# A gate folded into the last quarter of the output weights, and the last block stored in three pieces

## The chip, the cores and the metric
The kernel runs on one core of one Trainium2 chip. A core has TensorE (PE: matmuls, and the loads of their stationary operands, PEld), VectorE (DVE), ScalarE (ACT), GpSimd (POOL) and SyncE (SP); each runs its own instructions in order and they wait for one another by semaphores. SP, ACT and POOL also issue DMAs, which sixteen DMA engines carry out. The metric is the device time of one execution in microseconds (us). The kernel before took 1354.91 us, the median of three runs (1353.6 to 1355.62).

## The reference, cut to what matters
The program is a two-layer hybrid network over 256 latent tokens and 256 context tokens of width 1024: layer 0 mixes tokens with an mLSTM, layer 1 with latent attention, and each is followed by a gated feed-forward part with a short convolution. What the change touches is the very end, the feed-forward part of layer 1 for the latent tokens:

```python
def _conv_ffn(h, w_in, conv_w, conv_b, w_out):
    gate, up = jnp.split(h @ w_in, 2, axis=-1)
    return (jax.nn.silu(_dwconv(gate, conv_w, conv_b)) * up) @ w_out
...
        f = _conv_ffn(_modulate(x, ml[3], ml[4]), ffn_w_in[i], ffn_conv_w[i], ffn_conv_b[i], ffn_w_out[i])
        x = _layer_norm(ALPHA * x + ml[5] * f, ln_g[i, 1], ln_b[i, 1])
```

`ml[5]` is a row of 1024 numbers, one for each output column, that comes from the condition `c`. It multiplies the columns of `f`, and `f` is a product with `w_out`; so multiplying the columns of `w_out` by it beforehand gives the same. The layer norm then takes mean and variance over the 1024 columns of each token and applies `ln_g` and `ln_b`.

## The kernel before, in words
All values are 32-bit. A matmul operand is held as the sum of a rounded high part and the rest, its low part, and a product is made of three matmuls (`mm3`, lines 417 to 422): high by high, high by low, low by high. Weights arrive as tiles of 128x1024, called raw (512 KB). `Stream` brings them in the order of a fixed list: `_load` (line 291) issues the load on SP into a ring of buffers, nine of them in the last part; `_split` (line 317) lets ScalarE round the raw tile to the high part (line 339), and `low` (line 359) lets VectorE subtract that from the raw tile (line 361), after which the raw buffer is free for the next load. Ordinary weights take one of three buffers of the tag `w`, so that the split of one waits until TensorE is done with the weight three before. Those marked wide take two buffers of another tag (`wu` in the profile) and are split ahead. `use` (line 368) hands a weight out and splits up to `AHEAD` = 8 further ones.

The layers' instructions are written down in program order, and a scheduler then orders those of each engine by priority (program order) and by when it reckons them ready. DMAs are subject to it too. Instructions marked `pin` keep their order.

In the feed-forward part of layer 1, `ffn_in` (line 1533) goes over 22 pairs of weights `fin1`. For each, TensorE makes a product, ScalarE and VectorE fetch it from the accumulators, apply the convolution and the activation, and split the result into `act`. Then `outmm` (line 1468) multiplies the 22 activations by the 22 weights `fout1`, one of 128x1024 for each. The 256 tokens are two blocks (t = 0 and 1) of 128. Block 0 has two accumulators of 512 columns, block 1 has three, of 512, 256 and 256 (`acc4(True)`, line 1491). The first 16 weights are each used for both blocks. The last six (`TAIL`, line 64) are kept, and used for one accumulator after another, so that these are finished one by one: block 0 first, columns 768 to 1023 of block 1 last. Of the 22, the first 12 are ordinary and the last ten wide (`WIDE`, line 65).

`ln_rows` (line 1179) follows: for each chunk, it multiplies the accumulator by the gate (line 1189), adds `ALPHA` times the residual (line 1190) and takes the statistics (line 1192). When the chunks of a block are in, it combines the statistics (line 1194), takes the root on ScalarE (line 1196) and the reciprocal, and a small product `nm` (line 1199). In this last call (`fin` given) the second pass subtracts the mean and multiplies by `ln_g` (line 1207), multiplies by the reciprocal root and adds `ln_b` (line 1209), in halves of 512 columns, and stores each half (line 1214): the first from SP, the second from ScalarE. The first half of block 0 goes another way, over ScalarE and POOL (lines 1211 to 1213).

The rows of gates are in memory as `gd[l, c]`, written by VectorE and SP (lines 539 to 543). `bcast` (line 1171) loads one from POOL's queue into all 128 partitions. `mask` (line 472) is a tile of 128x256 that only the mLSTM of layer 0 reads.

Of the kernel before, what the change touches and what calls it, by code (L numbers as in the profile page):

```python
# [11 lines left out]
ALU = mybir.AluOpType  # L12
# [11 lines left out]
ALPHA = float((2 * DEPTH) ** 0.25)  # L24
# [7 lines left out]
CW = 1024  # L32
# [34 lines left out]
MWIDE = (3, 4, 5, 6)  # L67

YTAIL = 3


def _stat(w, m, kt0, nkt):
# [10 lines left out]
def _plan():  # L83
    ids, order = {}, []

    def add(key, cols, wide=False):
        if key not in ids:
            ids[key] = (len(ids), cols)
        order.append((key, wide))
# [28 lines left out]
    for n in ("y21", "y22", "yt4"):  # L118
        for j in range(6):
            if (n, j) == ("yt4", 6 - YTAIL):  # L120
                for c, m in enumerate((3, 3, 2)):
                    add(("dkv", 0, c), m * 320)
            add((n, 0, j), cols[j], n == "yt4" and j >= 6 - YTAIL)
    for c in range(2):
# [129 lines left out]
class Stream:  # L254
# [62 lines left out]
    def _split(self):  # L317
        k, j = self.k, self.ns
        key, wide = self.order[j]
        cols = self.ids[key][1]  # L320
        while self.nl <= j:
            self._load()
        self.nsum = max(self.nsum, j)
        while self.nsum < min(j + SUMS, self.n):
            while self.nl <= self.nsum:
                self._load()
            self._sum(self.nsum)
            self.nsum += 1
        raw = self.raw[j]
        if wide:  # L330
            h, l = self.unit(), None
            if self.later is None:
                l = self.unit()
        else:
            w = k.pool.tile([128, 2, CW], F32R, tag="w", name="w", bufs=NB)
            h, l = w[:, 0], w[:, 1]
            self.live.append(j)
        src = raw[:, :cols]
        k.behind(k.nc.scalar.copy(h[:, :cols], src), self.behind)  # L339
        if key[0] in ("vt2", "yt2"):  # L340
            k.nc.scalar.dma_start(k.t2d[key[0][0], key[1], key[2]][:, :cols], src)
        self.hl[j] = [h, l]
        self.ns += 1
        if l is None:
            self.later.append((j, src, self.hl[j]))
        elif key[0] == "dkv" and key[2]:
            self.kept_low.append((j, src, h, l))
        else:
            self.low(j, src, h, l)
        while self._room():  # L350
            self._load()
# [39 lines left out]
class K:  # L391
# [787 lines left out]
    def ln_rows(self, pss, xres, gate, fin=None):  # L1179

        nc = self.nc
        self.zs = zs = []
        for t in range(2):
            z = self.uf("z")
            st = self.tiny(6 * len(pss[t]), "st").rearrange("p (a b) -> p a b", b=6)
            for i, (ps, c) in enumerate(pss[t]):
                h = c.start // 512
                hc = slice(c.start - h * 512, c.stop - h * 512)
                nc.vector.tensor_tensor(z[:, c], ps, gate[h][:, hc], op=ALU.mult)
                nc.vector.scalar_tensor_tensor(z[:, c], xres[t][h][:, hc], ALPHA, z[:, c],  # L1190
                                               op0=ALU.mult, op1=ALU.add)
                nc.vector.bn_stats(st[:, i], z[:, c])
            mv = self.tiny(2, "mv")
            nc.vector.bn_aggr(mv, st)
            rs = self.tiny(1, "rs")
            nc.scalar.activation(rs, mv[:, 1:2], AF.Sqrt, bias=self.keps, scale=1.0)
            nc.vector.reciprocal(rs, rs)
            nm = self.tiny(1, "nm")
            nc.vector.scalar_tensor_tensor(nm, mv[:, 0:1], -1.0, rs, op0=ALU.mult, op1=ALU.mult)
            fine = len(pss[1]) > 2  # L1200
            if fin is not None:
                g, b, out = fin
                for c0, c1 in ((0, 512), (512, 1024)):
                    c, h = slice(c0, c1), c0 // 512
                    hc = slice(c0 - h * 512, c1 - h * 512)
                    if t or c0 == 512:
                        nc.vector.scalar_tensor_tensor(z[:, c], z[:, c], mv[:, 0:1], g[h][:, hc],
                                                       op0=ALU.subtract, op1=ALU.mult)
                        nc.vector.scalar_tensor_tensor(z[:, c], z[:, c], rs, b[h][:, hc], op0=ALU.mult, op1=ALU.add)
                    else:  # L1210
                        nc.scalar.activation(z[:, c], z[:, c], AF.Identity, bias=nm, scale=rs)
                        nc.gpsimd.tensor_tensor(z[:, c], z[:, c], g[h][:, hc], op=ALU.mult)
                        nc.gpsimd.tensor_tensor(z[:, c], z[:, c], b[h][:, hc], op=ALU.add)
                    (nc.scalar if c0 == 512 else nc.sync).dma_start(out[t * 128:(t + 1) * 128, c], z[:, c])
                yield
                continue
            cuts = (0,) if fine and t == 0 else (0, 256, 768) if fine else (0, 512)
            for a, b in zip(cuts, cuts[1:]):
                nc.vector.tensor_scalar(z[:, a:b], z[:, a:b], mv[:, 0:1], rs, op0=ALU.subtract, op1=ALU.mult)
            for a, b in ((0, 512), (512, 1024)) if len(cuts) == 1 else ((cuts[-1], 1024),):  # L1220
                nc.scalar.activation(z[:, a:b], z[:, a:b], AF.Identity, bias=nm, scale=rs)
            zs.append(z)
            yield
# [380 lines left out]
    def w_fout0(self, x1d, mid):  # L1604
# [119 lines left out]
        self.step(self.bg)  # L1724
        for i in range(6 - YTAIL):
            if i:
# [3 lines left out]
            if i == 0:  # L1730
                self.tick(1)
        st.limit = [x[0] for x in st.order].index(("yt4", 0, 6 - YTAIL))
        st.behind = []
# [3 lines left out]
        mid(None, None, None)  # L1737
        ws = [(i, st.use(("yt4", 0, i), hold=True)) for i in range(6 - YTAIL, 6)]
        for b in range(2):
# [315 lines left out]
def build(tc, off, a, out):  # L2055
    es = ExitStack()
    with es:
        k = K(tc, es, off, a)
        nc = k.nc
# [45 lines left out]
        gate = k.bcast(k.gd[0, 2][1:2, :], "gate")  # L2105
# [19 lines left out]
        gate = k.bcast(k.gd[0, 2][0:1, :], "gate")  # L2125
# [21 lines left out]
        def half(us):  # L2147
            return lambda i: tuple(us[i // 2][:, n, (i % 2) * 256:(i % 2 + 1) * 256] for n in range(2))
        hc, hl = half(hcu), half(hlu)
# [19 lines left out]
        hc = hcu = None  # L2169
# [16 lines left out]
        gate = k.bcast(k.gd[1, 2][0:1, :], "gate")  # L2186
# [9 lines left out]
        k.late.append(k.ln_x(2, k.zs, [x3d[0], x3d[1]]))  # L2196
        st.limit = st.n
        k.take_late()
        acts = k.ffn_in(1, None, 256, 1, pre, both=h1u)
        k.drain()  # L2200
        h1 = h1u = None
# [2 lines left out]
        gate = k.bcast(k.gd[1, 5][0:1, :], "gate")  # L2204
# [25 lines left out]
```

## Time and profile before
One execution was profiled. Its own time was 1355.75 us, at a granted clock of 0.999.

| | us |
|---|---|
| median of three runs | 1354.91 |
| the profiled execution | 1355.75 |
| its span, first to last instruction | 1353.9 |
| first matmul with an output weight `fout1` | 1284.75 |
| last matmul ends | 1345.96 |

Times inside the span count from its start. A line of the timeline gives start, duration, engine, line of the kernel and operation, the tiles written and read (`z<-y,gate`), their shapes and how many; in brackets, how long the engine was idle before and who released it. `ACTq`, `SPq` and `POOLq` are DMA issues of these engines. A line of busy time by stretches gives the stretch, its length, the busy time of PE, PEld, DVE, ACT and POOL with the number of instructions, the granted clock, the busy share of the sixteen DMA engines and what they moved in GB/s. A line of a group gives engine, operation, tiles, shape and number, then busy time in all, the mean in ns, and the idle time before. A line of one tile's operations gives their shortest, median and longest duration in ns and the first and last start in us. A line of waits gives who waited for whom: in total, how often, and the longest. A line of DMA issues gives the number, the size and the median us from issue to landing; a line of a DMA queue gives packets, MB and the share of the sixteen engines' time.

### The profile page before, as it was taken

How to read it: one execution, taken by the hardware profiler on the slowest of the kernel's cores; microseconds unless marked ns; L12 is line 12 of the kernel's file. 1: busy time of each engine (PE TensorE's matmuls, PEld its weight loads, DVE VectorE, ACT ScalarE, POOL GpSimd, SP SyncE). 2: the span in 40 equal slices, each digit the busy share in tenths (PEclk: the TensorE clock that was granted, in tenths of full speed). 3: DMA queues.
4: the chain of work that ended last, by engine and by line, in shares of the span. 5: the costliest groups of instructions: out<-in, count | busy, mean ns of one | idle time of the engine just before them, and what ended most of it. 6: DMA issues, size and time to landing. Idle time of an engine off the chain costs nothing.

```text
span 1353.9 us, 18752 instructions
## 1 busy us (share of the span) xinstructions
PE 1340.2 (99%) x6658; PEld 1120.0 (83%) x6658; DVE 1057.5 (78%) x1747; ACT 710.6 (52%) x1248; POOL 124.6 (9%) x218
## 2 busy tenths in 40 slices
PE   9999999999999999999999999999999999999997
PEld 6777888888888888888898888888878998988886
DVE  4787757578687696897979978767899788898873
ACT  4764534445734546374643334333557767576660
POOL 0122000011101011030001000000001002000100
PEclk9999999999999999999999999999999999999999
DMA  9888847889676374786627877746987437366750
GB/s 363 311 261 270 302 156 252 245 266 311 231 237 206 99 232 126 254 289 222 210 96 241 299 242 231 221 148 199 311 255 245 156 101 213 131 209 190 260 189 31
DMA packets 92493, 298.26 MB, mean 220 GB/s; under 512 B 12104, under 2 KB 16456, under 8 KB 92400
## 3 DMA queue, kind: packets, MB, share of 16 engines
q1 hardware_dynamic: 62848, 218.65, 48.8%
q0 software_dynamic: 17888, 58.09, 14.1%
q10 hardware_dynamic: 11664, 20.32, 4.1%
q8 instruction: 52, 0.85, 0.3%
q14 instruction: 41, 0.34, 0.1%
HBM read 263.56 MB, written 33.46 MB: 219 GB/s over the span
## 4 chain that ended last, share of the span: by engine, by line
PE 94%; DMA 2%; DVE 2%; ACT 1%; issue 0%; ACTq 0%; DVEq 0%; SPq 0%
PE fin L1448 8%; PE fin L421 6%; PE fin L420 6%; PE tok L420 6%; PE tok L422 6%; PE fin L422 6%; PE tok L421 6%; PE y L421 6%; PE y L422 6%; PE y L420 6%; PE qk L420 4%; PE qk L422 4%; PE qk L421 4%; PE up L696 2%; PE up L420 2%; PE up L422 1%
## 5 line engine op out<-in xcount | busy, mean ns | idle before, releaser
L361 DVE TENSOR_TENSOR w<-raw,w 128x1024 fp32r<-128x1024 f32 (+2 forms) x286 | 343.0, 1201 | 135.4 <-ACT w L339 132.5
L339 ACT CAST w<-raw 128x1024 fp32r<-128x1024 f32 (+2 forms) x286 | 296.3, 1037 | 288.4 <-PE fin L422 77.9
L532 DVE SCALAR_TENSOR_TENSOR junk<-ar,bc 128x1024 f32<-128x1024 f32 x128 | 155.7, 1216 | 4.1 <-ACT adav L547 1.1
L421 PE MATMUL fin<-h,w 128*128 128x512 f32 (+1 forms) x376 | 141.2, 376 | 0.0
L422 PE MATMUL fin<-h,w 128*128 128x512 f32 (+1 forms) x376 | 140.9, 375 | 0.0
L420 PE MATMUL fin<-h,w 128*128 128x512 f32 (+1 forms) x376 | 140.8, 376 | 0.1
L1448 PE MATMUL fin<-h,w 128*128 128x512 f32 (+1 forms) x640 | 112.1, 337 | 0.0
L1448 PEld LDWEIGHTS fin<-h,w 128*128 128x128 f32 x640 | 98.3, 190 | 13.3
L420 PE MATMUL qk<-xc,w 128*128 128x512 f32 x256 | 100.6, 393 | 0.0
L422 PE MATMUL qk<-xc,w 128*128 128x512 f32 x256 | 99.9, 390 | 0.0
L421 PE MATMUL qk<-xc,w 128*128 128x512 f32 x256 | 99.8, 390 | 0.0
L420 PEld LDWEIGHTS fin<-h,w 128*128 128x128 f32 x376 | 70.6, 188 | 13.2 <-ACT h L1284 0.3
L422 PEld LDWEIGHTS fin<-h,w 128*128 128x128 f32 x376 | 70.8, 188 | 12.8
L421 PEld LDWEIGHTS fin<-h,w 128*128 128x128 f32 x376 | 70.8, 188 | 12.8 <-DVE h L1285 0.2
L422 PEld LDWEIGHTS qk<-xc,w 128*128 128x128 f32 x256 | 48.1, 188 | 10.0
L421 PEld LDWEIGHTS qk<-xc,w 128*128 128x128 f32 x256 | 48.1, 188 | 9.7
L420 PEld LDWEIGHTS qk<-xc,w 128*128 128x128 f32 x256 | 48.1, 188 | 9.6
L420 PE MATMUL tok<-w,hT 128*128 128x512 f32 x128 | 49.9, 390 | 0.0
L422 PE MATMUL tok<-w,hT 128*128 128x512 f32 x128 | 49.8, 389 | 0.0
L421 PE MATMUL tok<-w,hT 128*128 128x512 f32 x128 | 49.8, 389 | 0.0
L361 DVE TENSOR_TENSOR wu<-raw,wu 128x1024 fp32r<-128x1024 f32 (+1 forms) x37 | 43.7, 1200 | 4.4 <-ACT wu L339 4.1
L713 ACT ACTIVATE fg<-fg 128x512 f32<-128x512 f32 (+1 forms) x44 | 23.1, 525 | 45.4 <-DVE fg L711 39.3
(475 smaller groups left out, 3104.7 us busy)
## 6 DMA issues: line engine op xcount, KB each, us to landing
raw<-in_ws SPq DMA_DIRECT2D x282, 512.0 KB, 4.6
ar<-in_adaT SPq DMA_DIRECT2D x80, 512.0 KB, 4.5
adaw<-in_ada SPq DMA_DIRECT2D x16, 512.0 KB, 8.2
t2d<-raw ACTq DMA_DIRECT2D x13, 512.0 KB, 5.7
raw<-t2d SPq DMA_DIRECT2D x13, 512.0 KB, 5.2
raw<-in_ws POOLq DMA_DIRECT2D x13, 512.0 KB, 7.3
zr<-fd ACTq DMA_DIRECT2D x33, 128.0 KB, 4.5
xmd<-xr POOLq DMA_DIRECT2D x16, 256.0 KB, 4.5
```

The costliest lines, as they stand in the source:

```text
L339: k.behind(k.nc.scalar.copy(h[:, :cols], src), self.behind)
L361: i = self.k.nc.vector.tensor_sub(l[:, :n], src, h[:, :n])
L420: mm(out, w[0], x[0], start=start, stop=False, skip_group_check=on)
L421: mm(out, w[0], x[1], start=False, stop=False, skip_group_check=on)
L422: mm(out, w[1], x[0], start=False, stop=stop, skip_group_check=on)
L532: nc.vector.scalar_tensor_tensor(o, w, 1.0, self.bc[j], op0=ALU.mult, op1=ALU.mult, accum_out=col[:, k, j:j + 1])
L696: nc.tensor.matmul(ps[m], w[k][i][:, c], hT[k][:, j], start=made[m] == 0, stop=made[m] == 23)
L713: nc.scalar.activation(tmp[:, :n], tmp[:, :n], AF.Silu)
L1448: self.nc.tensor.matmul(ps[:, 0:256] if x else ps, w[x][:, k * 128:(k + 1) * 128], h[:, 0:256] if x else h, start=i == 0, stop=i == 15)
```

## The change
There are three edits. While an output weight is prepared, VectorE multiplies columns 768 to 1023 of its raw tile by the gate, in place, ahead of the rounding. For that a quarter of the gate row is loaded into the mask tile, from POOL's queue, ahead of `ffn_in` in program order. In the last `ln_rows`, columns from 768 on are then only added to the residual, straight from the accumulator. For block 0 that cuts the second chunk in two, for block 1 it leaves out the multiplication of the third chunk. The second pass of block 1 subtracts and multiplies in halves as before, but first for both; multiplication by the root with the addition of `ln_b`, and the store, go in three pieces of 512, 256 and 256 columns, stored from SP, ScalarE and SP. `nm` is made for block 0 alone.

```diff
+GC = 768
...
         raw = self.raw[j]
+        if key[0] == "fout1":
+            k.nc.vector.tensor_tensor(raw[:, GC:], raw[:, GC:], self.gate, op=ALU.mult)
         if wide:
...
                 h = c.start // 512
-                hc = slice(c.start - h * 512, c.stop - h * 512)
-                nc.vector.tensor_tensor(z[:, c], ps, gate[h][:, hc], op=ALU.mult)
-                nc.vector.scalar_tensor_tensor(z[:, c], xres[t][h][:, hc], ALPHA, z[:, c],
-                                               op0=ALU.mult, op1=ALU.add)
+                e = min(c.stop, GC) if fin is not None else c.stop
+                for a, b in ((c.start, e), (max(e, c.start), c.stop)):
+                    if a < b:
+                        hc, x = slice(a - h * 512, b - h * 512), ps[:, a - c.start:b - c.start]
+                        if b == e:
+                            nc.vector.tensor_tensor(z[:, a:b], x, gate[h][:, hc], op=ALU.mult)
+                            x = z[:, a:b]
+                        nc.vector.scalar_tensor_tensor(z[:, a:b], xres[t][h][:, hc], ALPHA, x,
+                                                       op0=ALU.mult, op1=ALU.add)
                 nc.vector.bn_stats(st[:, i], z[:, c])
...
-            nm = self.tiny(1, "nm")
-            nc.vector.scalar_tensor_tensor(nm, mv[:, 0:1], -1.0, rs, op0=ALU.mult, op1=ALU.mult)
+            if fin is None or not t:
+                nm = self.tiny(1, "nm")
+                nc.vector.scalar_tensor_tensor(nm, mv[:, 0:1], -1.0, rs, op0=ALU.mult, op1=ALU.mult)
             fine = len(pss[1]) > 2
             if fin is not None:
                 g, b, out = fin
-                for c0, c1 in ((0, 512), (512, 1024)):
+                for c0, c1 in ((0, 512), (512, 1024)) if t else ((512, 1024),):
+                    nc.vector.scalar_tensor_tensor(z[:, c0:c1], z[:, c0:c1], mv[:, 0:1], g[c0 // 512],
+                                                   op0=ALU.subtract, op1=ALU.mult)
+                for c0, c1 in ((0, 512), (512, 768), (768, 1024)) if t else ((0, 512), (512, 1024)):
                     c, h = slice(c0, c1), c0 // 512
                     hc = slice(c0 - h * 512, c1 - h * 512)
                     if t or c0 == 512:
-                        nc.vector.scalar_tensor_tensor(z[:, c], z[:, c], mv[:, 0:1], g[h][:, hc],
-                                                       op0=ALU.subtract, op1=ALU.mult)
                         nc.vector.scalar_tensor_tensor(z[:, c], z[:, c], rs, b[h][:, hc], op0=ALU.mult, op1=ALU.add)
                     else:
...
         k.take_late()
+        st.gate = k.mask.rearrange("p a b -> p (a b)")
+        nc.gpsimd.dma_start(st.gate, k.gd[1, 5][0:1, GC:].to_broadcast([128, CW - GC]))
         acts = k.ffn_in(1, None, 256, 1, pre, both=h1u)
```

## The prediction
> **What bounds the kernel now.** I read the page first: the busy shares and the chain of work that ended last.
>
> ```profile
> span 1353.9 us, 18752 instructions
> ...
> PE 1340.2 (99%) x6658; PEld 1120.0 (83%) x6658; DVE 1057.5 (78%) x1747; ACT 710.6 (52%) x1248; POOL 124.6 (9%) x218
> ...
> PE 94%; DMA 2%; DVE 2%; ACT 1%; issue 0%; ACTq 0%; DVEq 0%; SPq 0%
> ```
>
> TensorE is busy for 1340.2 of 1353.9 us and holds 94% of the chain. So a change can do two things: shorten what follows the last matmul, or make TensorE wait before it. I take the end first, from the timeline after the last matmul.
>
> ```profile
> 1345.68 0.28 PE L422 MATMUL y<-wu,act 128*128 128x256 f32 x1
> 1346.00 0.42 DVE L1189 TENSOR_TENSOR z<-y,gate 128x256 f32<-128x256 f32 x1 [0.32 <-PE y L422]
> ...
> 1346.46 0.42 DVE L1190 SCALAR_TENSOR_TENSOR z<-xres,z 128x256 f32<-128x256 f32 x1
> 1346.92 0.43 DVE L1192 BATCH_NORM_STATS2 st<-z 128x6 f32<-128x256 f32 x1
> 1347.38 0.24 DVE L1194 BATCH_NORM_AGGREGATE mv<-st 128x2 f32<-128x18 f32 x1
> 1347.65 0.29 ACT L1196 ACTIVATE rs<-mv,keps 128x1 f32<-128x1 f32 x1 [4.29 <-DVE mv L1194]
> 1347.65 0.75 DVE L1207 SCALAR_TENSOR_TENSOR z<-z,mv,gr 128x512 f32<-128x512 f32 x1
> 1348.32 0.16 DVE L1197 RECIPROCAL rs<-rs 128x1 f32<-128x1 f32 x1
> 1348.39 0.73 DVE L1207 SCALAR_TENSOR_TENSOR z<-z,mv,gr 128x512 f32<-128x512 f32 x1
> ```
>
> ```profile
> 1349.04 0.15 DVE L1199 SCALAR_TENSOR_TENSOR nm<-mv,rs 128x1 f32<-128x1 f32 x1
> 1349.11 1.41 DVE L1209 SCALAR_TENSOR_TENSOR z<-z,rs,br 128x512 f32<-128x512 f32 x2
> 1349.88 0.34 SPq L1214 DMA_DIRECT2D out_dram<-z  x1
> 1350.55 0.34 ACTq L1214 DMA_DIRECT2D out_dram<-z  x1
> ```
>
> The last matmul ends at 1345.96. From there VectorE (DVE) works without a gap to 1350.52; only the square root, on ScalarE, is beside it, and it is hidden by the first of the L1207 operations. The two halves of the last block are stored from 1349.88 and 1350.55. How the stores move is in the busy share of the DMA engines:
>
> ```profile
> 1348.00:1350.60 2.60, 0.00 (x0) 0.00 (x0) 2.52 (x6) 0.00 (x0) 0.00 (x0) 1.00 0.00 0
> 1350.60:1352.20 1.60, 0.00 (x0) 0.00 (x0) 0.00 (x0) 0.00 (x0) 0.00 (x0) 0.69 0.87 328
> ```
>
> ```profile
> out_dram<-z ACTq DMA_DIRECT2D x2, 256.0 KB, 2.0
> ```
>
> In the 1.60 us the sixteen engines are busy 0.87 of the time: 1.39 us for both halves, 0.70 us for 256 KB. They begin after 1350.60 and stop by 1352.20, so data run from about 1350.8, some 0.9 us after the first issue, to about 1352.15 without a break. The second half, 0.67 us behind the first, arrives just as the first is through; it has landed 2.0 us after its issue. The transfer is thus limited by the engines from its beginning: what moves the end is **when the first piece is issued**, not the last.
>
> **The end, part by part.** (1) The last chunk (columns 768 to 1023 of block 1) loses the multiplication by the gate: 1346.46 − 1346.00 = **−0.46 us**, start to start. Nothing hides it: VectorE has been idle 0.32 us waiting for that matmul. Bounds 0.42 (its duration) and 0.46. (2) The small operation `nm` is no longer made for block 1: 1349.11 − 1349.04 = **−0.07 us** (bounds 0.07 and its duration, 0.15). (3) The L1207 pair and the first half of L1209 stay as they are, so the first piece is issued 0.53 us earlier, at 1349.35. (4) The second half of L1209 becomes two operations of 256 columns. Such operations take 0.42 to 0.48 us; before, the pair of 512 took 1.41, so an independent successor starts 0.67 after its predecessor, 0.08 before that ends. The last piece ends at 1348.58 + 0.67 + 0.40 + 0.48 = 1350.13 instead of 1350.52 and is issued at about 1350.16. With the same 0.9 us its data could move from 1351.06, while the first 384 KB keep the engines busy from 1350.25 to 1351.30. So it queues behind them, and the extra operation costs nothing: the cover is the transfer of the first two pieces, 0.24 us of room. (5) The bytes are the same 512 KB, 1.39 us, if bytes set the price; the packets of the last two pieces are half as long. The nearest rows are a stretch in which the ScalarE queue (q10) moves mostly 128 KB tiles and the SP queue (q1) mostly 512 KB ones, and two transfers of one queue:
>
> ```profile
> q1 hardware_dynamic: 2208, 6.80, 42.4%
> q10 hardware_dynamic: 5173, 6.02, 38.0%
> ```
>
> ```profile
> fd<-fg POOLq DMA_DIRECT2D x11, 256.0 KB, 3.1
> ...
> fd<-fg POOLq DMA_DIRECT2D x11, 128.0 KB, 2.9
> ```
>
> In those 47 us q1 took 0.424 × 47 / 6.80 = 2.93 us of all engines for a MB at 3.1 KB a packet, and q10 0.380 × 47 / 6.02 = 2.97 at 1.2 KB. Packet length costs next to nothing, so I take **0**. The other end, by the fd rows, is that half the bytes save only 0.2 us; at the extreme each 128 KB piece takes the 0.70 us of a 256 KB one: +0.70. Sum at the end: −0.46 − 0.07 = **−0.53 us**; bounds −0.61 and +0.17.
>
> The Trainium skill ("DMA: Bandwidth & Descriptors", Bandwidth) fits a DMA as about 2.0 us plus its bytes at 436 GB/s, and asks to batch DMAs up to 1 MiB. By the fit, counted from the last issue, the shorter last piece would give 0.39 + 0.30 = 0.69 us instead of 0.53; by the advice the split is a loss. The 2.0 us of the store's row above holds its 256 KB as well, not only a fixed part, so here the row decides.
>
> **Ahead of the end: the 22 multiplications.** Each output weight (512 KB, 128x1024) gets one more VectorE operation, 128x256 with both operands in on-chip memory, before ScalarE rounds it (L339) and VectorE subtracts (L361). The nearest row has the same form, 417 ns. In all 22 × 0.417 = 9.2 us. The question is whether they lie in idle time.
>
> ```profile
> L1569 DVE TENSOR_TENSOR fg<-fg,fs 128x256 f32<-128x256 f32 x22 | 9.2, 417 | 0.4 <-ACT fg L713 0.4
> ```
>
> ```profile
> 1279.20:1284.80 5.60, 5.60 (x34) 4.93 (x33) 4.79 (x9) 3.85 (x7) 1.10 (x2) 1.00 0.97 332
> 1284.80:1318.30 33.50, 33.50 (x182) 29.02 (x181) 25.96 (x26) 23.31 (x25) 0.00 (x0) 1.00 0.63 206
> 1318.30:1333.50 15.20, 15.20 (x79) 12.98 (x78) 0.00 (x0) 0.00 (x0) 0.00 (x0) 1.00 0.00 1
> ```
>
> From the first output matmul to the last split (1284.80 to 1318.30) VectorE is idle for 33.50 − 25.96 = 7.5 us, and then 15.2 us more. The weights come in two kinds. The last ten (k 12 to 21) have buffers of their own and are made ahead:
>
> ```profile
> 1314.79 3.50 DVE L361 TENSOR_TENSOR wu<-raw,wu 128x1024 fp32r<-128x1024 f32 x3 [1.33 <-ACT wu L339]
> ```
>
> ```profile
> 1329.22 0.40 PE L420 MATMUL y<-wu,act 128*128 128x512 f32 x1
> ```
>
> They are ready at 1318.3, and the tail that uses the last six begins at 1329.22. Even all 9.2 us laid end to end would finish at 1327.5. So they cost **0**, covered by 10.9 us of lead. The first twelve share three buffers and are tighter:
>
> ```profile
> 1281.21 1.22 DVE L361 TENSOR_TENSOR w<-raw,w 128x1024 fp32r<-128x1024 f32 x1
> ...
> 1283.51 1.23 DVE L361 TENSOR_TENSOR w<-raw,w 128x1024 fp32r<-128x1024 f32 x1 [0.41 <-ACT w L339]
> ```
>
> ```profile
> 1284.75 0.40 PE L420 MATMUL y<-w,act 128*128 128x512 f32 x1
> ...
> 1287.52 0.40 PE L420 MATMUL y<-w,act 128*128 128x512 f32 x1
> ```
>
> k 0 is split by 1282.43 and used at 1284.75; k 1 by 1284.74 and 1287.52. The **slack is 2.3 to 2.8 us**, and TensorE takes 2.77 us a weight. The new multiplication needs only the raw tile, not the split buffer, and raw tiles come nine ahead, so it can be done before the cast's turn. If it falls directly ahead of the cast it delays it by 0.42; if VectorE has just begun another split, by 1.22 + 0.42 = 1.64. Both are below 2.3, so I take **0**; bounds 0, and 12 × 0.42 = 5.0 us if TensorE paid for each of the twelve. Tightest is the last feed-forward period, 5.60 us with 4.79 busy: two multiplications make it 5.63. VectorE then falls behind by 0.03 us for one period, and catches up where its share is 25.96 of 33.50.
>
> A new wait stands behind this: VectorE now waits itself for a raw tile to land, with the subtractions of other weights queued behind it, and TensorE waits for those. Before, ScalarE had these waits:
>
> ```profile
> ACT wu L339 <- DMA raw<-in_ws: 4.1, 5, 1.6
> ```
>
> The longest was 1.6 us, again under the slack. Each raw buffer is freed about 0.4 us later, and the SP queue's next load with it; the lead above covers that.
>
> **The gate row's load.** One more DMA on POOL's queue, 128 KB. It is ready when the gate row is in memory (the mask tile is out of use long before):
>
> ```profile
> L542 SPq DMA_DIRECT2D gd<-adat x16: 275/340/742, 134.9 to 875.4; - x16
> L1175 POOL DMA_DIRECT2D gate<-gd x8: 546/546/892, 598.8 to 1274.2; - x8
> ```
>
> From 875.4 on, then, for 0.55 us of issue. Its first reader, a tile that lands up to nine weights (9 × 2.77 = 25 us) ahead of its use at 1284.75, comes near 1260 at the earliest. Where it is put early, the stores behind it on POOL's queue wait with it; TensorE waits for none of them at that place. Its 128 KB are 0.35 us of the DMA engines at the rate above. I take **0**, bounds 0 and +0.35. In block 0 one operation more (0.42 + 0.43 + 0.43 for 0.69 + 0.69) costs nothing: that block's work ends over 2 us ahead.
>
> **Sum.** Profiled execution: 1355.75 us, a span of 1353.9 and 1.85 around it; minus 0.53 is 1355.2. The median of the runs shown is 0.84 lower, 1354.91; minus 0.53 gives **1354.4 us**. About 0.2% (2.7 us) is what a measurement of this kernel can tell from no change, so this is the same.
>
> **Rivals.**
> A (62%): as worked out. Its own range is 1353.7 to 1355.1, since the runs before lie between 1353.6 and 1355.62.
> B (8%): a piece of a store costs per packet, not per byte. Then 1349.35 + 0.9 + 3 × 0.70 ends at 1352.35, which is 0.17 later than before: 1355.1. For it: the fd rows, 2.9 against 3.1 us. Against it: the q10 row. The Trainium skill's advice to batch (same page and section) speaks for this one.
> C (20%): slower. VectorE becomes the bound of the twelve weights in three buffers: a multiplication that waits for its tile holds up the subtraction behind it, and each weight then reaches TensorE 0.42 us late, 5.0 us in all: 1354.91 + 5.0 − 0.5 = 1359.4. It decides once a split ends more than 2.3 us later. For it: 5.63 us of work in a 5.60 us period and 4.1 us of waits for tiles; against it: the longest wait is 1.6, and the next 33 us have 7.5 us free.
> D (10%): faster, from elsewhere. The added load and operations shift the order in which queues are filled, and a transfer on which TensorE waits comes earlier. The page's 1353.9 − 1340.2 = 13.7 us without a matmul bounds it, 7.9 of them behind the last one; half of the other 5.8 is 2.9, so 1354.4 − 2.9 = 1351.5. Nothing in the profile shows such a shift.
> That the end does not move because the store hides it is excluded by the 0.00 DMA share up to 1350.60.
>
> **How the numbers follow.** Faster by over 0.2%: D, 10%. Slower by over 0.2%: C, 20%. Same: A and B, 70%. The range 1353.0 to 1357.0 holds A with the scatter of runs, B, and the part of C with stalls of up to 2.6 us; D and the rest of C, some 2 in 10, are left out.
>
> **What would show it.** Right: the output matmuls without idle time up to about 1346; the last block's chain without L1189 in its third chunk and 4.13 instead of 4.52 us long up to the end of the last piece; the first store issued 3.39 us after the last matmul (3.92 before); DMA engines busy without a break for 1.39 us. Step (5) is wrong if that stretch is longer; the multiplications' step is wrong if TensorE shows waits for w or wu after the first output matmul, or the last split ends after 1329. The prediction fails if the last matmul ends more than 1 us from 1346.

## The result, and the profile after

The changed kernel took 1360.48 us, the median of seven runs (1357.48 to 1361.96), against 1354.91 before: a ratio of **1.0035, 95% interval 1.0026 to 1.0045**, some 4.7 us slower. (The two medians are 5.6 us apart; the two profiled executions, 1360.48 and 1355.75, differ by 4.73.) The range foreseen ended at 1357.0. Forecast was no change; this is rival C's side.

The profiled executions say where. I start from the first output matmul in each, because the moment at which it comes moves by a few us from one profiled execution to the next (1283.1 to 1286.4 in those of this study), whatever was changed. The page of the changed kernel, its span and its chain of work:

```profile
span 1358.4 us, 18768 instructions
...
PE 85%; DMA 9%; DVE 3%; ACT 1%; issue 1%; ACTq 0%; SPq 0%; POOL 0%; DVEq 0%; POOLq 0%
```

DMA holds 9% of the chain where it had 2%. That is a chain of another kind, not 7% of lost time: it follows back from TensorE's last wait. The timeline of TensorE in the changed kernel, first the rows around its waits, then its last matmul:

```profile
1284.70 0.40 PE L424 MATMUL y<-w,act 128*128 128x512 f32 x1
1285.66 0.50 PE L425 MATMUL y<-w,act 128*128 128x512 f32 x1 [0.57 <-DVE w L365]
1286.00 0.40 PE L426 MATMUL y<-w,act 128*128 128x512 f32 x1
1286.23 0.40 PE L424 MATMUL y<-w,act 128*128 128x512 f32 x1
...
1291.11 0.39 PE L424 MATMUL y<-w,act 128*128 128x512 f32 x1
1292.52 0.50 PE L425 MATMUL y<-w,act 128*128 128x512 f32 x1 [1.02 <-DVE w L365]
...
1309.08 0.39 PE L424 MATMUL y<-w,act 128*128 128x512 f32 x1
1309.67 0.50 PE L425 MATMUL y<-w,act 128*128 128x512 f32 x1 [0.20 <-DVE w L365]
...
1315.11 0.39 PE L424 MATMUL y<-w,act 128*128 128x512 f32 x1
1317.60 0.50 PE L425 MATMUL y<-w,act 128*128 128x512 f32 x1 [2.10 <-DVE w L365]
...
1350.62 0.28 PE L426 MATMUL y<-wu,act 128*128 128x256 f32 x1
```

Line 425 is the matmul that needs a weight's low part, which VectorE's subtraction (now line 365) makes. It should start 0.23 us after the one of line 424; at k 0, 2, 8 and 10 it starts 0.73, 1.18, 0.36 and 2.26 us later than that, 4.53 in all, and the next matmul follows after 0.33 or 0.34 instead of 0.23 each time, 0.42 in all. From the first output matmul to the end of the last it is 1350.90 − 1284.70 = 66.20 us, against 1345.96 − 1284.75 = 61.21 before: **+4.99**, which these waits make up (4.95). The kernel before has no wait of TensorE in this stretch. From the last matmul to the end it is 1358.386 − 1350.902 = 7.48 us, against 1353.934 − 1345.963 = 7.97: **−0.49** (the page prints the span to tenths; these are from the trace itself). With the first output matmul 0.05 earlier, the span is 4.45 longer. The 0.28 that are missing from the 4.73 lie outside the span: the time of an execution is 2.09 us longer than its span here, and 1.82 before. All seven runs show it (2.06 to 2.14), and the section on the experiments comes back to it.

What VectorE did meanwhile stands in the changed kernel's waits over the last stage (who waited for whom: us, times, longest):

```profile
DVE raw L333 <- DMA raw<-in_ws: 12.5, 10, 2.3
ACT wu L343 <- DVE raw L333: 12.2, 8, 2.9
...
PE y L425 <- DVE w L365: 3.9, 4, 2.1
```

VectorE stands 12.5 us in front of multiplications (line 333) whose tile has not landed. Before, VectorE had no such wait, and ScalarE had 4.1 us of them. The chain of the changed kernel just ahead of the first wait shows what queues behind:

```profile
1277.00 1.14 DVE w L365
1278.16 5.46 DMA raw<-in_ws
...
1283.65 0.42 DVE raw L333
1284.07 0.40 DVE fg L715
1284.47 1.14 DVE w L365
...
1285.63 4.85 DMA raw<-in_ws
1290.48 0.02 issue
1290.51 0.42 DVE raw L333
1290.93 0.40 DVE fg L715
1291.33 1.13 DVE w L365
```

The multiplication at 1283.65 is the eighth of the 22, that of k 7. Its tile is used some twenty us later, but the scheduler has put it, as I read it, where the tile was reckoned to land. Behind it in VectorE's order come a convolution step (line 715) and the subtraction for **k 0**, whose low part TensorE needs at 1284.93. That subtraction frees a raw buffer only at its end; from there the next load takes 4.85 us to land, and a multiplication waits for that one too. So the chain turns: subtraction, load, wait, multiplication, subtraction. The tile of k 9 holds up the subtraction of k 2 in the same way, 6.9 us later. VectorE's own rows at k 0, the multiplication and the subtraction:

```profile
1283.65 0.42 DVE L333 TENSOR_TENSOR raw<-raw,mask 128x256 f32<-128x256 f32 x1 [2.10 <-DMA raw<-in_ws]
...
1284.39 1.22 DVE L365 TENSOR_TENSOR w<-raw,w 128x1024 fp32r<-128x1024 f32 x1
```

The subtraction of k 0 begins at 1284.39 instead of 1281.21, 3.18 us later, and 2.10 of these are this one wait.

### The profile page after: what moved, and what is told of

It reads as the page before. It is cut to its first block, busy times and chain, and to the rows that moved or that the text cites. A ratio compares the mean times of both kernels' runs of the same rounds, so it can differ in the third digit from the quotient of the medians.

```text
span 1358.4 us, 18768 instructions
## 1 busy us (share of the span) xinstructions
PE 1341.5 (99%) x6658; PEld 1119.6 (82%) x6658; DVE 1064.0 (78%) x1769; ACT 709.4 (52%) x1248; POOL 125.2 (9%) x219
## 3 DMA queue, kind: packets, MB, share of 16 engines
q0 software_dynamic: 17936, 58.23, 14.1%
## 4 chain that ended last, share of the span: by engine, by line
PE 85%; DMA 9%; DVE 3%; ACT 1%; issue 1%; ACTq 0%; SPq 0%; POOL 0%; DVEq 0%; POOLq 0%
PE fin L1459 6%; PE fin L424 6%; PE tok L424 6%; PE fin L425 6%; PE fin L426 6%; PE tok L425 6%; PE tok L426 6%; PE qk L424 4%; PE qk L426 4%; PE qk L425 4%; DMA raw<-in_ws 4%; PE y L425 4%; PE y L426 4%; PE y L424 4%; DMA adaw<-in_ada 2%; PE up L424 2%
## 5 line engine op out<-in xcount | busy, mean ns | idle before, releaser
L343 ACT CAST wu<-raw 128x1024 fp32r<-128x1024 f32 (+1 forms) x37 | 37.4, 1040 | 15.3 <-DVE raw L333 12.2
```

## The experiments

A table of all runs first. The stretches are read off the one profiled execution of each as above, the end of the span to hundredths; the ratio is that of the runs against the kernel before on the same chip.

| kernel | first to last output matmul, us | last matmul to end, us | ratio, 95% interval |
|---|---|---|---|
| before | 61.21 | 7.97 | |
| changed | 66.20 | 7.48 | 1.0035 (1.0026 to 1.0045) |
| e1_behind | 61.22 | 7.48 | 0.9999 (0.9990 to 1.0008) |
| e2_wait_alone | 64.76 | 7.49 | 1.0023 (1.0013 to 1.0034) |
| e3_pool | 65.70 | 7.49 | 1.0040 (1.0026 to 1.0053) |
| e4_end_alone | 61.22 | 7.95 | 1.0003 (0.9994 to 1.0012) |
| e5_just_ahead | 61.22 | 7.49 | 0.9996 (0.9987 to 1.0005) |
| e6_wide_only | 61.68 | 7.49 | 1.0008 (0.9999 to 1.0017) |
| e7_ordinary_only | 63.76 | 7.49 | 1.0019 (1.0009 to 1.0028) |
| e9_halves | 61.21 | 7.43 | 1.0001 (0.9992 to 1.0010) |
| e10_ordinary_late | 62.74 | 7.48 | 1.0014 (1.0005 to 1.0023) |
| e11_wide_late | 63.13 | 7.49 | 1.0024 (1.0013 to 1.0035) |
| e12_ordinary_j5 | 61.22 | 7.49 | 0.9994 (0.9985 to 1.0004) |

My theory was that VectorE, which works in order, is held at multiplications put too early; the rival, that 22 operations are too much load for it.

**e1_behind.** The multiplications all stay; only their place in VectorE's order changes.

```diff
-            k.nc.vector.tensor_tensor(raw[:, GC:], raw[:, GC:], self.gate, op=ALU.mult)
+            i = k.nc.vector.tensor_tensor(raw[:, GC:], raw[:, GC:], self.gate, op=ALU.mult)
+            k.behind(i, [self.lows[j - 5]])
...
-        i = self.k.nc.vector.tensor_sub(l[:, :n], src, h[:, :n])
+        i = self.lows[j] = self.k.nc.vector.tensor_sub(l[:, :n], src, h[:, :n])
```

> The changed kernel with one ordering edge more: on VectorE the multiplication of weight j comes behind the subtraction of weight j-5, so that its tile has landed long before its turn. The multiplications themselves, 22 of 0.42 us, stay. Theory (in-order wait): VectorE's 12.5 us of waits for raw tiles fall below 2 us, TensorE's four waits in the output matmuls (4.5 us) go, the last matmul ends within 0.5 us of 1346, and the time is about 0.4 us below the kernel before, ratio 0.9997. Rival (VectorE's load of 9.2 us is too much): the waits of TensorE stay and the ratio stays near 1.0035.

The multiplications (shortest, median and longest duration, first and last start), first in the changed kernel, then in this one, and this one's wait:

```profile
L333 DVE TENSOR_TENSOR raw<-raw,mask x22: 415/422/428, 1260.6 to 1321.2; 128x256 f32<-128x256 f32 x22
```

```profile
L334 DVE TENSOR_TENSOR raw<-raw,mask x22: 415/419/426, 1269.9 to 1323.1; 128x256 f32<-128x256 f32 x22
```

```profile
DVE raw L334 <- DMA raw<-in_ws: 0.8, 1, 0.8
```

The same 22 operations of 0.42 us now begin 16.5 us before the first output matmul (1286.44 here) instead of 24.1, and find their tiles in place but for one wait of 0.8 us. TensorE has no wait, 61.22 us. The last matmul ended at 1347.66, not within 0.5 us of 1346 as expected: the output matmuls began 1.7 us later in this execution, which is why I read stretches. The time is that of the kernel before; the gain at the end is in the trace, 7.48 against 7.97 us, but cannot be told in the ratio. The rival falls: the full load is there, and TensorE waits for none of it.

**e2_wait_alone.** The converse: the wait stays, most of the load goes.

```diff
-            k.nc.vector.tensor_tensor(raw[:, GC:], raw[:, GC:], self.gate, op=ALU.mult)
+            k.nc.vector.tensor_tensor(raw[:, GC:GC + 1], raw[:, GC:GC + 1], self.gate[:, 0:1], op=ALU.mult)
```

> The changed kernel with each of the 22 multiplications cut to one column (128x1 in place of 128x256), which leaves the gate out of columns 769 to 1023; the waits for the raw tiles stay where they are, the load falls from 9.2 to about 2 us. Theory (in-order wait): VectorE still waits about 10 us for raw tiles, TensorE still 3 to 5 us, ratio 1.002 to 1.0035. Rival (VectorE's load): TensorE's waits are gone, ratio 0.9997.

```profile
L333 DVE TENSOR_TENSOR raw<-raw,mask x22: 150/159/161, 1259.1 to 1318.2; 128x1 f32<-128x1 f32 x22
```

```profile
DVE raw L333 <- DMA raw<-in_ws: 14.1, 12, 2.3
...
PE y L425 <- DVE w L365: 2.4, 3, 1.2
```

With 22 × 0.16 = 3.5 us of work instead of 9.2, VectorE still waits 14.1 us and the output matmuls still lose 64.76 − 61.21 = 3.55 of the 4.99 us. With the waits and 38% of the work, 71% of the loss is there. The rest goes with the 5.7 us of work that were taken away; that this work costs because it comes after a wait, when no slack is left, is argued and not shown.

**e3_pool.** The multiplication on another engine.

```diff
-            k.nc.vector.tensor_tensor(raw[:, GC:], raw[:, GC:], self.gate, op=ALU.mult)
+            k.nc.gpsimd.tensor_tensor(raw[:, GC:], raw[:, GC:], self.gate, op=ALU.mult)
```

> The changed kernel with the 22 multiplications on POOL instead of VectorE. Each still waits for its raw tile and still comes ahead of the rounding, and it takes longer there (1.4 us for 512 columns in the trace of before, so some 0.75 us for 256), but what queues behind it is not VectorE's work. Theory (in-order wait on VectorE): VectorE has no wait for raw tiles, TensorE none in the output matmuls, ratio 0.9997. Rival (each raw tile is done and freed later, so the loads run late): TensorE's waits stay or grow, ratio 1.003 or more.

```profile
L333 POOL TENSOR_TENSOR raw<-raw,mask x22: 732/852/1740, 1261.0 to 1320.5; 128x256 f32<-128x256 f32 x22
```

```profile
ACT wu L343 <- POOL raw L333: 14.3, 7, 5.0
```

My theory's number missed: 65.70 us, 1.0040. VectorE is free of the wait for landing, but it has moved to ScalarE, which now stands up to 5.0 us in front of the rounding of a wide weight, with the ordinary weights' roundings queued behind. I read it as the same fault on another queue, with the longer operation on top; this run does not part these two.

**e4_end_alone.** The last pass's edits without the multiplication of weights: the diff of the change, less the lines that make and use `self.gate`, and with `e = c.stop` for every chunk.

> The kernel before with the second half of the change alone: block 1's second pass and store in three pieces and nm left out for it; the gate stays in the last pass, no multiplication of weights. Theory: without the 0.46 us of the gate's multiplication what is left is the 0.07 us of nm, against some 0.1 us that the transfer of smaller pieces takes longer (1.48 against 1.39 us in the traces); from the last matmul to the end 7.9 to 8.0 us against 7.94 before, ratio 1.000. Rival (three pieces bring the gain by themselves, since the last one is short): 7.5 us or less. If smaller pieces cost per packet: 8.5 us.

7.95 us from the last matmul to the end, against 7.97, as foreseen: three pieces and the missing `nm` alone bring next to nothing. The gain of 0.49 us comes from the multiplication that is gone.

**e5_just_ahead.** The latest place (the edit is shown against e1_behind).

```diff
-            k.behind(i, [self.lows[j - 5]])
+            k.behind(i, [self.lows[j - (5 if wide else 1)]])
```

> As e1_behind, but for the twelve ordinary weights the multiplication comes as late as it can: behind the subtraction of the weight just before (j-1; the ten wide ones stay at j-5), so that it lies directly ahead of its own rounding. This tries the price that the prediction put on that place: a delay of 0.42 us or little more for each weight against 2.3 us of slack. If the prediction was right there: no wait of TensorE, 61.2 us from the first to the last output matmul (61.21 before, 66.2 changed). If the chain multiply, round, subtract is too long for the 2.77 us that a weight has, the lag grows from weight to weight, and the stretch is over 62.5 us.

```profile
ACT w L345 <- DVE raw L334: 11.9, 10, 1.8
```

ScalarE now waits for ordinary multiplications, up to 1.8 us each, and yet TensorE loses nothing: 61.22. The slack that the prediction relied on, 2.3 us, was enough for this.

**e6_wide_only and e7_ordinary_only.** The two kinds of weights apart.

```diff
-        if key[0] == "fout1":
+        if key[0] == "fout1" and wide:
```

(and `not wide` for e7_ordinary_only)

> The changed kernel with the multiplication for the ten wide weights alone (k 12 to 21), which leaves the gate out of the other twelve in the last quarter of the columns. The theory reads the trace of the changed kernel so that the waits at k 0 and k 2 (about 2.1 us with the slower matmul after each) come from multiplications of ordinary weights, and those at k 8 and k 10 (about 2.8 us) from those of wide ones. Then the output matmuls take 61.2 + 2.8 = 64.0 us. If the waits at k 8 and k 10 are a late result of the earlier ones, it is near 61.2. If only the sum of the load counts: 61.2 + 5.0 x 10/22 = 63.5 us, with the waits spread.

> The changed kernel with the multiplication for the twelve ordinary weights alone (k 0 to 11), which leaves the gate out of the other ten in the last quarter of the columns. Theory: the waits at k 0 and k 2 stay, those at k 8 and k 10 go; 61.2 + 2.1 = 63.3 us for the output matmuls. If the later waits are a late result of the earlier ones, all four stay, 66 us.

TensorE's waits with the ordinary ones alone, and in the same kernel ScalarE's for wide tiles:

```profile
1286.45 0.51 PE L425 MATMUL y<-w,act 128*128 128x512 f32 x1 [0.77 <-DVE w L365]
...
1293.48 0.50 PE L425 MATMUL y<-w,act 128*128 128x512 f32 x1 [1.18 <-DVE w L365]
```

```profile
ACT wu L343 <- DMA raw<-in_ws: 7.6, 6, 2.2
```

The ordinary ones cost 2.55 us, near the 2.1 expected, at the same two places. The wide ones alone cost 0.47 and not 2.8, another miss: I had read the waits at k 8 and k 10 as theirs, and they are not by themselves. Apart the two make 3.0, together 4.99. With only ordinary multiplications, the wide tiles already come later for ScalarE (7.6 us of waits, 4.1 before): late subtractions would free raw buffers late. That suggested an order of cause, which the next runs try.

**e10_ordinary_late, e11_wide_late, e12_ordinary_j5.** All 22 multiplications, the ordering edge for one kind alone (again shown against e1_behind).

```diff
-            k.behind(i, [self.lows[j - 5]])
+            if not wide:
+                k.behind(i, [self.lows[j - 1]])
```

(`if wide` with j − 5 for e11_wide_late, `if not wide` with j − 5 for e12_ordinary_j5)

> The changed kernel, all 22 multiplications in full, with the ordering edge of e5_just_ahead (behind the subtraction of j-1) for the twelve ordinary weights alone; the ten wide ones stay where the changed kernel has them. The groups apart gave 0.5 us (wide alone) and 2.6 us (ordinary alone) and together 5.0, so 1.9 us came from both at once. Theory: the waits of the ordinary multiplications make the loads of the wide tiles late, and only then do the wide multiplications hold VectorE up; with the ordinary ones out of the way the output matmuls take about 61.7 us, as in e6_wide_only. Rival: the full load of 22 is what turns the wide ones' waits into TensorE's; then 63 us or more.

> The counterpart: the edge (behind j-5) for the ten wide weights alone, the twelve ordinary ones as in the changed kernel. Theory: the waits at k 0 and k 2 stay, and the 1.9 us of both at once goes with the wide ones' waits; about 63.8 us, as in e7_ordinary_only. Rival (the full load): 65 us or more.

> As e10_ordinary_late, with the edge of the twelve ordinary weights at j-5 instead of j-1; the ten wide ones free as in the changed kernel. It asks why e10_ordinary_late took 62.7 us and not 61.7: if the place directly ahead of the rounding used up slack that the wide ones' waits then needed, the earlier place gives it back and the output matmuls take 61.2 to 61.9 us. If the wide ones' waits cost this much once all 22 multiplications are there, it stays at 62.5 us or more.

With the wide ones out of the way, 63.13 us where I expected 63.8: 1.92 of loss remain, near e7_ordinary_only. With the ordinary ones at j − 1, 62.74: 1.53 remain, which neither theory had named. With them at j − 5, nothing remains, though VectorE still waits for wide tiles:

```profile
DVE raw L334 <- DMA raw<-in_ws: 3.9, 4, 1.5
```

So the ordinary multiplications are what starts it, and once they are in a good place the wide ones' waits of at most 1.5 us fit into the slack. (In e6_wide_only, where the longest such wait was 2.1 us, 0.47 us were lost.) In e10_ordinary_late, then, the place directly ahead of the rounding had used that slack up. Either use of it is free alone (e5_just_ahead, e12_ordinary_j5); both together cost.

**e9_halves.** The store again in two halves, on top of e1_behind.

```diff
-                for c0, c1 in ((0, 512), (512, 768), (768, 1024)) if t else ((0, 512), (512, 1024)):
+                for c0, c1 in ((0, 512), (512, 1024)):
```

> As e1_behind, with block 1's last pass and store in two halves again instead of three pieces. The prediction held that the moment of the first issue sets the end, since the engines then move 512 KB without a break. If so, the halves lose nothing: from the last matmul to the end 7.40 to 7.45 us (7.44 with three pieces, 7.94 before). If the last piece's issue sets the end: three pieces are the better, and halves take 7.6 us or more. The time as a whole: ratio 0.9997, not to be told from 1.

Its issues, and the DMA engines while they move the block (the last but one figure is their busy share), in this kernel and, below, in the changed one with three pieces:

```profile
1349.53 0.34 SPq L1227 DMA_DIRECT2D out_dram<-z  x1
1350.19 0.34 ACTq L1227 DMA_DIRECT2D out_dram<-z  x1
```

```profile
1350.20:1352.20 2.00, 0.00 (x0) 0.00 (x0) 0.00 (x0) 0.00 (x0) 0.00 (x0) 0.71 0.70 262
```

```profile
1354.90:1357.00 2.10, 0.00 (x0) 0.00 (x0) 0.16 (x1) 0.00 (x0) 0.00 (x0) 0.50 0.71 250
```

The last matmul ended at 1346.14 here, so the first issue comes 3.39 us after it, and the end 7.43 us, against 7.48 with three pieces (the expectation's 7.44 and 7.94 take the span to tenths). The halves lose nothing; the third piece costs 0.05 us. The engines are busy for 2.00 × 0.70 = 1.40 us, and for 2.10 × 0.71 = 1.49 us with three pieces, 1.45 to 1.50 over all the kernels that store three.

No version beats the kernel before by what can be told: e12_ordinary_j5 (0.9994) and e5_just_ahead (0.9996) have intervals that hold 1. Over half of the 0.49 us of the end is lost again outside the span. Before, time and span differ by 1.82 or 1.83 us in the mean of each set of runs; in the changed kernel and in every version with multiplications on VectorE by 2.09 to 2.12, whether ten, twelve or 22 of them, and with the halves too. In e3_pool it is 1.84 and in e4_end_alone 1.96. So some 0.2 us of gain are left, 0.02% of the time. What makes the difference outside the span no run shows.

## Why the prediction was wrong

**The end: right, with one term mis-sized.** The gate's multiplication and `nm` went as worked out, and the second pass's additions begin 2.58 us after the last chunk's first operation instead of 3.11, 0.53 earlier. The rows of the changed kernel:

```profile
1350.94 0.42 DVE L1199 SCALAR_TENSOR_TENSOR z<-xres,y 128x256 f32<-128x256 f32 x1 [0.45 <-PE y L426]
...
1353.52 1.54 DVE L1220 SCALAR_TENSOR_TENSOR z<-z,rs,br 128x512 f32<-128x512 f32 x3
```

That the first issue sets the end held (e9_halves), and so did the three pieces bringing nothing (e4_end_alone). Step (5) put the packets' length at 0; the engines were busy for 0.05 to 0.11 us more, and the end came 0.05 us later than with halves. So the end gained 0.49 and not 0.53. By the fit of the Trainium skill ("DMA: Bandwidth & Descriptors", Anatomy of one DMA — SWDGE (gpsimd) path), which is given for DMAs issued from POOL, the estimate was 0.69; the traces of these stores from SP and ScalarE do not agree with it, since here the transfer's start and not its last piece's size decides. Left out of the sum was a change of the time outside the span, which was carried over as 1.85 us; it came out 0.28 us longer.

**The load of 22 operations: right.** e1_behind, e5_just_ahead and e12_ordinary_j5 have all 9.2 us of it and lose nothing. The delay of 0.42 us directly ahead of the rounding is inside the slack, as was said.

**The step that failed** is the "new wait": "The longest was 1.6 us, again under the slack." I took the waits that ScalarE had before as the size of those that VectorE would get. But they were the waits of an operation that stands at a weight's turn, whereas the multiplication needs nothing but the tile, and I had myself noted that "raw tiles come nine ahead". Put by a scheduler where its tile is reckoned to land, it waits for many of the loads: ten waits in 22, 12.5 us, the longest 2.3. The slack of 2.3 us was then set against the wrong sum: at k 0 a wait of 2.10, the multiplications and the lag of earlier ones made 3.18 us together. I used the early place to show that it would be out of the way of the rounding, and did not ask what then stood behind it: the subtractions of weights up to seven earlier. Nor did I follow the loop: late subtraction, late free buffer, late load, next wait. "Each raw buffer is freed about 0.4 us later ... the lead above covers that" was true of the load of work and not of the wait.

**Rival C** had the right side, 20%, and named this queue. Its 5.0 us come out close to the 4.99 measured, but that is luck, for it got there by another way: twelve times 0.42 against four waits of 0.4 to 2.3 us. Its point of decision, a split that ends over 2.3 us late, was the right one to look at.

**The gate row's load** went as the prediction allowed. Timeline of POOL in the changed kernel:

```profile
878.23 0.55 POOL L2211 DMA_DIRECT2D mask<-gd  x1 [12.19 <-DMA gd<-adat]
882.28 0.54 POOL L1604 DMA_DIRECT2D fd<-fg  x1 [3.51 <-DVE fg L1580]
```

It was put early and held POOL for 12.2 us, and the next store still waited for VectorE afterwards. Whether it cost a few tenths of a us before the first output matmul cannot be seen, since that moment moves by more; but the mean spans of e1_behind, e5_just_ahead, e9_halves and e12_ordinary_j5 lie 0.2 to 0.9 us below those of the kernel before, so it cannot have cost much. Rival D did not appear.

## What to carry to other kernels

An operation that is added ahead of work and needs only a loaded tile is ready the moment that tile lands, so a scheduler may put it right there; on an engine that works in order, everything behind it then waits for that DMA. Ask not only how long it takes and whether the engine has room, but what stands behind it and how far ahead of its use it may be put. If the kernel has slack at the turn of use, tie the operation to that turn, as one ordering edge did here.

## What the runs showed of the hardware

The first matmul after a wait of TensorE is shown with 0.50 us instead of 0.39, and the next starts after 0.33 or 0.34 instead of 0.23. At four waits that was 0.42 us, beside the waits themselves. A 128x256 multiplication of 32-bit numbers took 0.42 us on VectorE and a median of 0.85 on POOL (0.73 to 1.74). Moving 512 KB to memory took 1.39 to 1.40 us in rows of 2 KB and 1.45 to 1.50 when half of it went in rows of 1 KB. The Trainium skill ("DMA: Bandwidth & Descriptors", Why small descriptors are slow) gives a fixed cost of about 3 cycles for each packet beside one for each 32 bytes; an estimate from it, with the 850 MHz that the page gives for the fabric, is 0.03 us for 256 KB at half the length, and the traces show 0.05 to 0.11.
